# A written order for VectorE and ScalarE in the opening and around each LayerNorm

## Chip, cores and metric

The kernel runs on one core of a Trainium2 chip. The metric is the device time of one execution in microseconds. The engines are TensorE (PE: matmuls, with weight loads as PEld), VectorE (DVE), ScalarE (ACT), GpSimd (POOL) and SyncE (SP, which issues most DMAs).

## The reference

A trunk of two post-norm layers on 256 tokens of 2048 features, in float32. The input passes a LayerNorm first. Each layer projects its input once (`w_in`) into latents for queries and keys (`zq`, `zk`) and into a gated unit `u`, runs latent attention with rotary positions on one half and a 31-tap depthwise convolution with its own LayerNorm on the other, and joins both in one product (`w_out`, the kernel's `wo`). A LayerNorm, a squared-ReLU MLP and another LayerNorm follow:

```
u = u + b_glu
h = u[..., :CONV_WIDTH] * jax.nn.sigmoid(u[..., CONV_WIDTH:])
h = causal_depthwise_conv(h, w_dw, b_dw)
h = jax.nn.silu(layer_norm(h, g_cln, b_cln))
mix = jnp.concatenate([attn, h], axis=-1) @ w_out
x = layer_norm(ALPHA * x + mix, ln1_g, ln1_b)
f = jnp.square(jax.nn.relu(x @ w1)) @ w2
return layer_norm(ALPHA * x + f, ln2_g, ln2_b)
```

## The kernel before

**Precision and chunks.** Each float32 factor is split into a high part, a cast to fp32r on ScalarE, and a low part, the difference, on VectorE or, for some chunks, GpSimd. A product is three matmuls: high by high, low by high, high by low. Weights stream from HBM in chunks of up to 1 MB in a fixed plan: SP loads chunk i to a slot `wr` (`load_next`), `cutting` makes `wh` and `wl` of it in pieces, and `retire` gives the slots back after the last matmul. `pump` cuts as far ahead as `ahead` and `cap` let it.

**The token side.** The 256 tokens are two tiles (t = 0, 1) of 128 rows, each in four column blocks of 512 (n = 0 to 3). A `Norm` object holds a LayerNorm: `stats` and `head` make mean and reciprocal deviation (the power runs on GpSimd), `nrm` normalises a block, `turn` transposes it on TensorE (`tri`, `tra`, `trb`) and splits it to `xTi`, `xTa` or `xTb`. On VectorE a block costs two SCALAR_TENSOR_TENSOR. On GpSimd's path, `nrm` with `nc.gpsimd`, two ACTIVATE of ScalarE (L410, L411) and two GpSimd operations (L412, L413) do it. `First` is the norm of the input (name `i`): gain and bias are applied after the transposes, column by column (`xv`), on VectorE for those in the set `GV` and on ScalarE (L497) otherwise.

**LayerNorms.** LN a follows `wo`, LN b the MLP's second product `w`. `close` computes the last column blocks of a product and does the first steps of the norm between them (`between`): blocks 0 and 1 of tile 0 on VectorE, block 2 on GpSimd's path, and for tile 1 blocks 1 to 3 there too. `after_norm` writes the rest, and then the first product that reads it: `u` behind the input's norm and LN b, the MLP's `f` behind LN a; `lag` is the number of chunks that tile 0 runs ahead. While it writes the norm, `hold` keeps `pump` from cutting chunks, and `gate` puts the cuts that follow behind the split of block 0 of tile 1.

**What sets the order.** A scheduler of the tile framework orders each engine's instructions from the written program and its dependences. It may move an instruction that is ready by its own reckoning ahead of an earlier written one, except where `tc.issue_after` binds the pair. `beside` runs a generator's steps between the matmuls that follow. A loaded slot's DMA waits for the slot's last reader.

**The opening.** SP loads the input, the first four `u` chunks (wr0 to wr3), small parameters (`gbr`), the convolution's taps (`wdr`), a bias and then the four `zq` chunks wr4 to wr7. The norm of the input is written tile by tile with the cuts of the `u` chunks between (`ready_tile`), and `angles_within_pi` (GpSimd) and `rope_tables` (ScalarE: Abs, Sin, Cos) around the first products. `conv_norm` transposes the convolution's result (`yT`), applies gain, bias and SiLU on ScalarE (`th`, `zz`) and splits it to `mc`, while `wo`'s products of the attention half (`mx`) run.

Of the kernel before, what the change touches and what calls it, by code (L numbers as in the profile page):

```python
# [16 lines left out]
P = 128  # L17
# [34 lines left out]
GV = {(t, n, k) for t, n in ((1, 0), (1, 1), (0, 2)) for k in range(4)} | {(0, 0, 2), (0, 0, 3)}  # L52
# [24 lines left out]
def hybrid_trunk(ctx: ExitStack, tc: tile.TileContext, x, positions, inv_freq, ln_in_g, ln_in_b,  # L77
# [3 lines left out]
    clock = dict(pe=0.0, dve=0.0)  # L81

    class Counted:

        def __init__(self, eng, key, cost):
            self.eng, self.key, self.cost = eng, key, cost
# [26 lines left out]
    vector = Counted(nc.vector, "dve", dve_cost)  # L113

# [55 lines left out]
    def split(hi, lo, src):  # L170
        return nc.scalar.copy(hi, src), vector.tensor_sub(lo, src, hi.bitcast(F32))  # L171
# [59 lines left out]
    raws, ready, cut_after, last = {}, {}, {}, {}  # L231
    state = dict(loaded=0, cut=0, retired=0, ahead=1, cap=5, hold=False, gate=None, pieces=2)
# [15 lines left out]
    def cutting(pieces):  # L248
# [108 lines left out]
    def rstd_of(var, eps, scale, name):  # L357
# [3 lines left out]
        nc.gpsimd.tensor_tensor(out=r, in0=v, in1=mhalf, op=ALU.pow)  # L361
        return r

    class Norm:
# [35 lines left out]

        def nrm(self, t, n, eng=None):
# [7 lines left out]
            if eng is nc.gpsimd:  # L409
                nc.scalar.activation(X[:, t, c], a, AF.Identity, bias=self.nmu(t), scale=1.0)  # L410
                nc.scalar.activation(X[:, t, c], X[:, t, c], AF.Copy, scale=r)  # L411
# [28 lines left out]
    def after_norm(N, keys, ps, lag):  # L440
# [11 lines left out]
        N.nrm(1, 0)  # L452
        N.turn(1, 0)
        gate = N.cut
        N.nrm(0, 3)
        N.turn(0, 3)
        for n in range(1, NC4):
            N.nrm(1, n)
            N.turn(1, n)
# [4 lines left out]
        state.update(hold=False, gate=gate)  # L464
# [11 lines left out]
        state["gate"] = None  # L476


    class First(Norm):
# [9 lines left out]
        def gain(self, ps, t, n):  # L489
            v = work(f"xv{t}{n}", "ev", 4)  # L490
            for k in range(4):
# [4 lines left out]
                else:  # L496
                    nc.scalar.activation(v[:, c], ps[:, c], AF.Identity, bias=b, scale=g)  # L497
# [49 lines left out]
    nc.scalar.copy(gbT, ps[:, 0:32])  # L547

    def ready_tile(t, n):
        N.nrm(t, n)  # L550
        N.turn(t, n)

# [3 lines left out]
    first = cutting(4)  # L556
    next(first)
    next(first)
    ready_tile(0, 0)
    state["gate"] = N.cut[:1]  # L560
    beside(first)
    state["gate"] = None
    ready_tile(0, 1)
    for n in range(NC4):
        N.stats(1, n)
    N.head(1)
    ready_tile(1, 0)
    for n in range(1, NC4):
        for _ in cutting(4):
            pass  # L570
        if n + 1 < NC4:
            ready_tile(0, n + 1)
        ready_tile(1, n)
# [12 lines left out]
    def parameters():  # L586
# [3 lines left out]
        nc.scalar.copy(pT.rearrange("p l r -> p (l r)"), ps[:, 0:NR * L])  # L590
        nc.scalar.mul(pH.rearrange("p l r -> p (l r)"), ps[:, 0:NR * L], 0.5)
        for l in range(L):
# [4 lines left out]
            nc.scalar.copy(wdT[:, l].rearrange("p c k -> p (c k)"), ps[:, 0:8 * CK])  # L597
# [28 lines left out]
    def rope_tables():  # L626
        af, tmp = angles[:, 0], angles[:, 3]
        nc.scalar.activation(tmp, af, AF.Abs)
        nc.scalar.activation(sinT.rearrange("p a b -> p (a b)"), af, AF.Sin)
        nc.scalar.activation(cosT.rearrange("p a b -> p (a b)"), tmp, AF.Sin, bias=hpi, scale=-1.0)  # L630
# [14 lines left out]
    def convolve(l, i, h, ca):  # L645

        acc = [psumc(f"cv{l}{i}{j}", j)[:, :S] for j in range(2)]
        for j in range(2):
            c = 2 * i + j
            nc.scalar.activation(acc[j], h[:, c], AF.Identity, bias=pT[:, l, 32 + c:33 + c],  # L650
# [9 lines left out]
        for j in range(2):  # L660
            nc.scalar.copy(ca[:, 2 * i + j], acc[j])
# [4 lines left out]
    def out_part(ps, tag, l, k0, n, kc, act, last, tokens=(0, 1), amid=None):  # L666

        hi, lo = get(tag, l, k0, n, kc)
        for t in tokens:
            for ki in range(4):  # L670
# [46 lines left out]
    def close(tag, l, k0, act, N, first=False):  # L717

        def between(i, ps):
            if i == 0:  # L720
                accumulate(0, ps, NC4 - 1, first, N)
                N.head(0)
                N.nrm(0, 2, nc.gpsimd)
                N.nrm(0, 0)
                N.nrm(0, 1)
            elif not N.last:
                N.turn(0, 0)
# [27 lines left out]
        for n in range(1, NC4):  # L755
            if not N.last or n == 2:
                N.nrm(1, n, nc.gpsimd)

    for l in range(L):
# [8 lines left out]
        after_norm(N, [("u", l, 0, kc) for kc in range(4)], ps, 3 if l else 1)  # L768
        xT = N.xT

        def gate0(ps):
            for t in range(2):
# [3 lines left out]
                nc.scalar.activation(th[:, :256], ub[:, 256:], AF.Tanh, scale=0.5)  # L776
# [7 lines left out]
                nc.scalar.mul(hg[:, 0:2, t * P:(t + 1) * P], v3(px[:, 0:256], 2), 0.5)  # L784
# [5 lines left out]
        if l == 0:  # L790
            angles_within_pi()
# [22 lines left out]
        def rms_T(z, n, gb_, dst, name):  # L814
            r, cn = [], []
            ss = [sm.tile([P, 1], F32, name=f"ss{name}{t}", tag="ss") for t in range(2)]
            for t in range(2):
                jk = work(f"jk{name}{t}", "rp", 2)
                nc.scalar.activation(jk[:, :n], z[t][:, :n], AF.Square, accum_out=ss[t])
# [24 lines left out]
        def u_group(i):  # L844
# [402 lines left out]
```

## Time and profile before

| | |
|---|---|
| median of 3 runs | 2027.1 us (2026.82 to 2027.65) |
| profiled execution | 2029.86 us |
| its span | 2027.7 us |
| mean granted TensorE clock | 0.993 of full |
| TensorE busy | 1993.4 us, 98% of the span |
| VectorE, ScalarE, GpSimd busy | 60%, 47%, 16% |

The page gives busy times by engine and by group of instructions. The list of TensorE's waits says for which engine it stood and how long. A timeline gives start, duration, engine, line, operation, output and inputs of consecutive equal instructions (xN for how many), with the idle time ahead and what ended it in brackets. All helper calls on TensorE and VectorE have one line, L93, so they are told apart by tile names.

### The profile page before, as it was taken

How to read it: one execution, taken by the hardware profiler on the slowest of the kernel's cores; microseconds unless marked ns; L12 is line 12 of the kernel's file. 1: busy time of each engine (PE TensorE's matmuls, PEld its weight loads, DVE VectorE, ACT ScalarE, POOL GpSimd, SP SyncE). 2: the span in 40 equal slices, each digit the busy share in tenths (PEclk: the TensorE clock that was granted, in tenths of full speed). 3: DMA queues.
4: the chain of work that ended last, by engine and by line, in shares of the span. 5: the costliest groups of instructions: out<-in, count | busy, mean ns of one | idle time of the engine just before them, and what ended most of it. 6: DMA issues, size and time to landing. Idle time of an engine off the chain costs nothing. (4 is left out here: it accounts for less than half of the span.)

```text
span 2027.7 us, 26190 instructions
## 1 busy us (share of the span) xinstructions
PE 1993.4 (98%) x10542; PEld 1706.2 (84%) x10542; DVE 1224.7 (60%) x1725; ACT 947.7 (47%) x1341; POOL 332.4 (16%) x208
## 2 busy tenths in 40 slices
PE   7999999999999999999999999999999999999998
PEld 5999778888888888888879997788888888888886
DVE  6875787554555555455567747865555545555564
ACT  5456455543453354344345564554434434443441
POOL 2287802000000000000038763200000000000001
PEclk8999999999999999999999999999999999999999
DMA  7465745456555645657556555455564565556562
GB/s 234 150 175 176 244 166 207 151 200 211 166 187 189 226 153 195 213 167 249 166 167 176 139 174 208 167 187 186 188 227 148 189 201 191 184 190 227 181 224 74
DMA packets 226169, 377.67 MB, mean 186 GB/s; under 512 B 15954, under 2 KB 70082, under 8 KB 225024
## 3 DMA queue, kind: packets, MB, share of 16 engines
q1 hardware_dynamic: 225696, 375.47, 56.6%
q8 instruction: 82, 1.34, 0.3%
q10 hardware_dynamic: 352, 0.54, 0.1%
q14 instruction: 39, 0.32, 0.1%
HBM read 373.88 MB, written 2.10 MB: 185 GB/s over the span
## 5 line engine op out<-in xcount | busy, mean ns | idle before, releaser
L264 ACT CAST wh<-wr 128x1024 fp32r<-128x1024 f32 (+2 forms) x700 | 684.9, 1031 | 744.5 <-DVE wl L93 316.8
L93 DVE TENSOR_TENSOR wl<-wr,wh 128x1024 fp32r<-128x1024 f32 (+1 forms) x592 | 694.2, 1216 | 432.5 <-ACT wh L264 294.1
L93 PE MATMUL f<-xTa,wh 128*128 128x512 f32 x1920 | 676.7, 398 | 0.0
L93 PE MATMUL w<-wh,h 128*128 128x512 f32 x2048 | 632.1, 389 | 1.5 <-DVE f015s L93 1.5
L93 PE MATMUL f<-xTa,wl 128*128 128x256 f32 x1920 | 538.0, 281 | 0.0
L93 PEld LDWEIGHTS w<-wh,h 128*128 128x128 f32 x2048 | 384.5, 188 | 81.8 <-DVE f015s L93 1.8
L93 PEld LDWEIGHTS f<-xTa,wh 128*128 128x128 f32 x1920 | 360.4, 188 | 87.6
L93 PE MATMUL w<-wl,h 128*128 128x512 f32 x1024 | 398.5, 389 | 0.0
L93 PEld LDWEIGHTS f<-xTa,wl 128*128 128x128 f32 x1920 | 362.7, 189 | 0.9
L265 POOL TENSOR_TENSOR wl<-wr,wh 128x1024 fp32r<-128x1024 f32 (+1 forms) x108 | 245.0, 2291 | 85.5 <-ACT wh L264 42.2
L361 POOL TENSOR_TENSOR rb<-vb,mhalf 128x1 f32<-128x1 f32 x4 | 3.7, 923 | 1397.6 <-DVE nmub L93 1397.6
L93 PEld LDWEIGHTS w<-wl,h 128*128 128x128 f32 x1024 | 192.2, 188 | 39.6
L93 DVE SCALAR_TENSOR_TENSOR cv<-hg,wdT,cv 128x255 f32<-128x255 f32 (+14 forms) x480 | 187.2, 464 | 11.4 <-ACT cv L650 11.4
L93 PE MATMUL wo<-wh,mx 128*128 128x512 f32 x256 | 83.9, 401 | 1.0 <-ACT mx L171 1.0
L93 PE MATMUL wo<-wh,mc 128*128 128x512 f32 x256 | 79.7, 391 | 0.0
L93 PE MATMUL u<-xTi,wh 128*128 128x256 f32 x384 | 71.3, 286 | 0.0
L93 PE MATMUL u<-xTb,wh 128*128 128x256 f32 x384 | 71.2, 286 | 0.0
L93 DVE TENSOR_TENSOR X<-X,w 128x512 f32<-128x512 f32 x44 | 30.2, 687 | 64.6 <-PE w L93 64.6
L93 PEld LDWEIGHTS u<-xTi,wh 128*128 128x128 f32 x384 | 60.3, 191 | 0.2
L93 PEld LDWEIGHTS u<-xTb,wh 128*128 128x128 f32 x384 | 60.3, 192 | 0.2
L93 PEld LDWEIGHTS wo<-wh,mx 128*128 128x128 f32 x256 | 48.7, 191 | 11.6 <-ACT mx L171 1.5
L93 PEld LDWEIGHTS wo<-wh,mc 128*128 128x128 f32 x256 | 48.1, 188 | 9.9
(403 smaller groups left out, 1812.6 us busy)
## 6 DMA issues: line engine op xcount, KB each, us to landing
wr<-in_w_dram SPq DMA_DIRECT2D x256, 1024.0 KB, 5.2
wr<-in_w_out_dram SPq DMA_DIRECT2D x32, 1024.0 KB, 5.0
wr<-in_w_in_dram SPq DMA_DIRECT2D x60, 512.0 KB, 4.2
wr<-in_w_in_dram SPq DMA_DIRECT2D x8, 1024.0 KB, 11.0
wr<-in_w_uq_dram SPq DMA_DIRECT2D x24, 256.0 KB, 4.1
wr<-in_w_in_dram SPq DMA_DIRECT2D x8, 640.0 KB, 4.5
wr<-in_w_ukv_dram SPq DMA_DIRECT2D x8, 512.0 KB
wr<-in_w_in_dram SPq DMA_DIRECT2D x16, 128.0 KB, 5.1
```

The lines of the kernel that those rows point to most:

```text
L93: return f(*args, **kw)
L264: nc.scalar.copy(hi[:, c], raw[:, c])
L265: low = eng.tensor_sub(lo[:, c], raw[:, c], hi[:, c].bitcast(F32))
L361: nc.gpsimd.tensor_tensor(out=r, in0=v, in1=mhalf, op=ALU.pow)
```

## The change

1. `Counted` can chain an engine: while its name is in `chained`, each instruction issued through `vector` or `scalar` comes behind the one written before it. In the opening both engines are chained, and the steps stand in a list: `n` normalises, `t` transposes and splits, `c` cuts a piece of a `u` chunk, `s` makes the statistics of tile 1.
2. `hold` and `gate` are gone. VectorE makes every block of LN a and LN b (two operations each, `first` and `second`), in a written order, and is chained from the start of `close`'s last steps to the end of the norm. GpSimd's path is left to the last norm alone. The cuts of other chunks are not part of the lists.
3. `GV` holds the fourth column of each block and one more.
4. `angles_within_pi` comes behind the power of the query latents' norm, `rope_tables` behind the key latents.
5. The first `lag` is 2. The matmuls of `wo`'s second attention chunk for tile 1, and the first of the next chunk, are bound to earlier `yT` transposes.
6. By the order on SP, `gq` is loaded ahead of wr5 and `gk` ahead of wr6. SP's rows down to wr4 are unchanged.

The diff, cut to its core (everywhere else `nc.scalar` becomes `scalar`):

```diff
-GV = {(t, n, k) for t, n in ((1, 0), (1, 1), (0, 2)) for k in range(4)} | {(0, 0, 2), (0, 0, 3)}
+GV = {(t, n, 3) for t in range(2) for n in range(4)} | {(0, 0, 2)}
...
                 clock[self.key] += self.cost(op, args, kw)
-                return f(*args, **kw)
+                with ExitStack() as order:
+                    if self.key in chained and self.prev is not None:
+                        order.enter_context(tc.issue_after(self.prev.ins))
+                    self.prev = f(*args, **kw)
+                return self.prev
...
             with ExitStack() as order:
-                for ins in state["gate"] or ():
-                    order.enter_context(tc.issue_after(ins.ins))
                 for ins in cut_after.get(i, ()):
                     order.enter_context(tc.issue_after(ins.ins))
-                nc.scalar.copy(hi[:, c], raw[:, c])
+                scalar.copy(hi[:, c], raw[:, c])
...
-        while not state["hold"] and state["cut"] < min(state["loaded"], upto):
+        while state["cut"] < min(state["loaded"], upto):
...
+        def first(self, t, n):
+            c = slice(n * 512, (n + 1) * 512)
+            a = self.source(t, n)
+            vector.scalar_tensor_tensor(out=a, in0=a, scalar=self.mv[t][0][:, 0:1], in1=self.g[:, c],
+                                        op0=ALU.subtract, op1=ALU.mult)
...
+        def steps(self, text):
+
+            for w in text.split():
+                dict(f=self.first, s=self.second, t=self.turn)[w[0]](int(w[1]), int(w[2]))
...
-        state["hold"] = True
-        for n in range(3):
-            N.nrm(0, n)
-            N.turn(0, n)
...
-        gate = N.cut
...
+        if not isinstance(N, First):
+            N.steps("t01 f02 s02 f10 s10 t02 f11 t10 s11 f03 t11 s03 f12 s12 t03 t12")
+            pump(index[keys[3]] + 1)
+            N.steps("f13 s13 t13")
+        chained.clear()
         for kc in range(lag):
             for _ in mm(0, kc):
                 pass
             tick()
-        state.update(hold=False, gate=gate)
...
+    chained.update(("dve", "act"))
     for n in range(NC4):
         N.stats(0, n)
     N.head(0)
...
+    chunk = [cutting(4) for _ in range(4)]
+
+    for step in "n00 n01 c0 t00 c0 c0 c0 s t01 c1 n02 c1 n10 c1 n11 c1 t10 t02 c2 c2 n03 c2 c2 n12 t11 t03 c3 c3 n13 c3 c3 t12 t13".split():
...
+    for c in chunk:
+        beside(c)
+    chained.clear()
...
             if i == 0:
+                if not N.last:
+                    chained.add("dve")
                 accumulate(0, ps, NC4 - 1, first, N)
                 N.head(0)
-                N.nrm(0, 2, nc.gpsimd)
-                N.nrm(0, 0)
-                N.nrm(0, 1)
...
+                else:
+                    N.steps("f00 f01")
             elif not N.last:
-                N.turn(0, 0)
+                N.steps("s00 s01 t00")
...
+        behind["wo", l, 8, 0, 0, 1] = turned[2]
+        with tc.issue_after(turned[0].ins):
+            out_part(ps, "wo", l, 0, 3, 1, mixT, True, (0,))
         with tc.issue_after(turned[1].ins):
-            out_part(ps, "wo", l, 0, 3, 1, mixT, True, (0,))
-        with tc.issue_after(turned[2].ins):
             out_part(ps, "wo", l, 0, 3, 1, mixT, True, (1,))
```

How the order moves, at three places. In the names, wh4 and wh5 are the high parts of the first two `zq` chunks, wh3 that of the last `u` chunk, xv02 and xv12 the columns of block 2 of tiles 0 and 1; both tiles of a block share one buffer, `xTi1` for block 1.

ScalarE in the opening, before, from the splits of blocks 2, 3 and 1 to the first `zq` casts:

```order
L171 CAST xTi2_243<-xv02_249 128x4x128
L171 CAST xTi3_280<-xv03_286 128x4x128
L171 CAST xTi1_196<-xv11_262 128x4x128
L590 COPY pT_331<-prmT_456 128x80
L591 ACTIVATE pH_332<-prmT_456 128x80
L497 ACTIVATE xv12_299<-tri12_294,gbT_157 128x128 x4
L497 ACTIVATE xv13_322<-tri13_317,gbT_157 128x128 x4
L171 CAST xTi2_243<-xv12_299 128x4x128
L171 CAST xTi3_280<-xv13_322 128x4x128
L264 CAST wh4_426<-wr4_346 128x1024 x2
L264 CAST wh5_536<-wr5_372 128x1024 x2
```
And now, from the third `u` chunk on:

```order
L98 CAST wh2_257<-wr2_140 128x512 x4
L98 ACTIVATE xv11_274<-tri11_269,gbT_157 128x128 x3
L98 CAST wh4_426<-wr4_346 128x1024 x2
L98 CAST xTi1_206<-xv11_274 128x4x128
L98 ACTIVATE xv03_287<-tri03_282,gbT_157 128x128 x3
L98 CAST wh5_511<-wr5_384 128x1024 x2
L98 CAST xTi3_281<-xv03_287 128x4x128
L98 CAST wh3_294<-wr3_143 128x512 x4
L98 ACTIVATE xv12_310<-tri12_305,gbT_157 128x128 x3
```
The casts of wr4 and wr5 came behind every split of the norm; now they stand ahead of the splits of block 1 of tile 1 and block 3 of tile 0, and the last `u` chunk's casts (wh3) come behind them.

ScalarE at LN a of layer 0, before; wr47 belongs to this group of the MLP, tra000 holds the transposes of block 0 of tile 0:

```order
L264 CAST wh47_3072<-wr47_3056 128x1024 x2
L410 ACTIVATE X_70<-X_70,nmua00_3031 128x512
L411 ACTIVATE X_70<-X_70,ra00_3029 128x512
L171 CAST xTa00_3084<-tra000_3085 128x4x128
L171 CAST xTa01_3122<-tra001_3123 128x4x128
```
And now; wr49 is the first chunk of the next group of the MLP:

```order
L98 CAST wh47_3064<-wr47_3048 128x1024 x2
L98 CAST wh48_3159<-wr48_3062 128x1024 x2
L98 CAST wh49_3186<-wr49_3157 128x1024 x2
L98 CAST xTa00_3078<-tra000_3079 128x4x128
L98 CAST xTa01_3102<-tra001_3103 128x4x128
L98 CAST wh51_3264<-wr51_3242 128x1024 x2
L98 CAST xTa02_3114<-tra002_3115 128x4x128
```
ScalarE's two normalising passes (L410, L411) are gone, and the casts of wr48, wr49 and wr51 stand ahead of the splits of blocks 0 and 2.

VectorE at the same place, before; `ga0`, `ba0` are gain and bias, `wo0_8_3_1` the last product of `wo`:

```order
L93 SCALAR_TENSOR_TENSOR X_70<-X_70,mva00_3025,ga0_2786 128x512 x3
L93 BN_STATS sta01_2785<-X_70 128x6
L93 SCALAR_TENSOR_TENSOR X_70<-X_70,ra00_3029,ba0_2787 128x512 x3
L93 TENSOR_TENSOR X_70<-X_70,wo0_8_3_1_3041 128x512
L93 BN_STATS sta01_2785<-X_70 128x6
L93 TENSOR_TENSOR xTa00_3084<-tra000_3085,xTa00_3084 128x4x128
L93 TENSOR_TENSOR xTa01_3122<-tra001_3123,xTa01_3122 128x4x128
```
And now:

```order
L98 SCALAR_TENSOR_TENSOR X_70<-X_70,mva00_3025,ga0_2786 128x512 x2
L98 TENSOR_TENSOR X_70<-X_70,wo0_8_2_1_2937 128x512
L98 BN_STATS sta01_2785<-X_70 128x6
L98 TENSOR_TENSOR wl47_3065<-wr47_3048,wh47_3064 128x1024 x2
L98 SCALAR_TENSOR_TENSOR X_70<-X_70,ra00_3029,ba0_2787 128x512 x2
L98 TENSOR_TENSOR wl49_3187<-wr49_3157,wh49_3186 128x1024 x2
L98 TENSOR_TENSOR xTa00_3078<-tra000_3079,xTa00_3078 128x4x128
L98 TENSOR_TENSOR X_70<-X_70,wo0_8_3_1_3033 128x512
```
The passes over gain and bias are two and two rather than three and three, and low halves of wr47 and wr49 stand between them and ahead of the first split's subtraction, which now comes ahead of the last accumulation.

## Rows read from the trace of the kernel before

**Rows 1.** The page: span, and busy time of the engines.

```profile
span 2027.7 us, 26190 instructions
...
PE 1993.4 (98%) x10542; PEld 1706.2 (84%) x10542; DVE 1224.7 (60%) x1725; ACT 947.7 (47%) x1341; POOL 332.4 (16%) x208
```

**Rows 2.** TensorE's waits: instruction, releaser; us in total, times, longest.

```profile
PE tri L93 <- DVE xv L93: 7.5, 2, 4.3
...
PE yT L93 <- ACT zz L1080: 2.2, 4, 0.9
```

**Rows 3.** Timeline, TensorE, opening: start, us, instruction, [idle before, releaser].

```profile
29.45 1.12 PE L93 MATMUL tri<-ident,X 128*128 128x128 f32 x4 [4.28 <-DVE xv L93]
...
53.75 0.48 PE L93 MATMUL zq<-wh,xTi 128*128 128x512 f32 x1
```

**Rows 4.** Windows: us, busy of each engine, PEclk, DMA share, GB/s.

```profile
30.00:35.00 5.00, 2.98 (x13) 2.29 (x12) 4.95 (x12) 4.00 (x11) 0.81 (x3) 0.50 0.98 323
...
256.00:260.00 4.00, 4.00 (x12) 3.08 (x12) 2.79 (x5) 4.00 (x8) 0.00 (x0) 0.57 1.08 409
...
300.00:307.00 7.00, 7.00 (x33) 5.79 (x32) 6.72 (x12) 1.45 (x2) 3.33 (x3) 1.00 0.17 42
```

**Rows 5.** Timeline, VectorE, opening.

```profile
25.30 2.81 DVE L93 TENSOR_TENSOR wl<-wr,wh 128x512 fp32r<-128x512 f32 x4
...
28.04 3.90 DVE L93 TENSOR_SCALAR xv<-tri,gbT 128x128 f32<-128x128 f32 x12
...
45.64 2.36 DVE L93 TENSOR_TENSOR wl<-wr,wh 128x1024 fp32r<-128x1024 f32 x2 [4.72 <-ACT wh L264]
```

**Rows 6.** Timeline, SyncE's queue and ScalarE, opening.

```profile
26.00 0.61 SPq L543 DMA_DIRECT2D wdr<-in_w_dw_dram  x2
...
27.61 4.93 SPq L244 DMA_DIRECT2D wr<-in_w_in_dram  x3
...
25.75 2.18 ACT L264 CAST wh<-wr 128x512 fp32r<-128x512 f32 x4 [0.75 <-DMA wr<-in_w_in_dram]
...
38.89 1.22 ACT L171 CAST xTi<-xv 128x512 fp32r<-128x512 f32 x2
...
44.55 2.00 ACT L264 CAST wh<-wr 128x1024 fp32r<-128x1024 f32 x2 [4.44 <-DMA wr<-in_w_in_dram]
```

**Rows 7.** DMA issues of the MLP's weights: count, KB each, us to landing.

```profile
wr<-in_w_dram SPq DMA_DIRECT2D x256, 1024.0 KB, 5.2
```

**Rows 8.** Timelines at LN a, layer 0: SyncE's queue, TensorE, ScalarE.

```profile
304.64 3.65 SPq L244 DMA_DIRECT2D wr<-in_w_dram  x3
...
307.17 0.60 PE L93 MATMUL tra<-ident,X 128*128 128x128 f32 x4
...
310.82 0.73 PE L93 MATMUL f<-wh,xTa 128*128 128x512 f32 x2 [0.96 <-DVE xTa L93]
...
307.81 0.59 ACT L171 CAST xTa<-tra 128x512 fp32r<-128x512 f32 x1 [3.25 <-PE tra L93]
```

**Rows 9.** Timelines at LN a, layer 1: SyncE's queue, TensorE.

```profile
1299.14 3.65 SPq L244 DMA_DIRECT2D wr<-in_w_dram  x3
...
1305.25 0.73 PE L93 MATMUL f<-wh,xTa 128*128 128x512 f32 x2 [0.62 <-DVE xTa L93]
```

**Rows 10.** Timelines at LN b, layer 0: SyncE's queue, VectorE, TensorE.

```profile
1021.28 3.96 SPq L244 DMA_DIRECT2D wr<-in_w_in_dram  x4
...
1027.09 0.68 DVE L93 TENSOR_TENSOR xTb<-trb,xTb 128x512 fp32r<-128x512 f32 x1
...
1027.82 0.73 PE L93 MATMUL u<-wh,xTb 128*128 128x512 f32 x2 [1.09 <-DVE xTb L93]
```

**Rows 11.** Timeline, TensorE, the yT transposes of layer 0.

```profile
252.55 1.07 PE L93 MATMUL yT<-ident,yt 128*128 128x128 f32 x5
...
255.54 0.44 PE L93 MATMUL yT<-ident,yt 128*128 128x128 f32 x2 [0.47 <-ACT zz L1080]
...
255.73 0.48 PE L93 MATMUL wo<-wh,mx 128*128 128x512 f32 x1
```

More of the change, by code (lines that the diff above doesn't have):

```diff
@@ L80, in hybrid_trunk @@
     nc = tc.nc
-    clock = dict(pe=0.0, dve=0.0)
+    clock = dict(pe=0.0, dve=0.0, act=0.0)
+    chained = set()
     class Counted:
         def __init__(self, eng, key, cost):
-            self.eng, self.key, self.cost = eng, key, cost
+            self.eng, self.key, self.cost, self.prev = eng, key, cost, None
         def __getattr__(self, op):
@@ L113, in hybrid_trunk @@
     vector = Counted(nc.vector, "dve", dve_cost)
+    scalar = Counted(nc.scalar, "act", lambda op, args, kw: 0.0)
     cst = ctx.enter_context(tc.tile_pool(name="cst", bufs=1))
@@ L230, in hybrid_trunk @@
     index = {k: i for i, (k, _) in enumerate(plan)}
-    raws, ready, cut_after, last = {}, {}, {}, {}
-    state = dict(loaded=0, cut=0, retired=0, ahead=1, cap=5, hold=False, gate=None, pieces=2)
+    raws, ready, cut_after, behind, last = {}, {}, {}, {}, {}
+    state = dict(loaded=0, cut=0, retired=0, ahead=1, cap=5, pieces=2)
     def load_next(pieces=False):
@@ L360, in rstd_of @@
         r = sm.tile([P, 1], F32, name=f"r{name}", tag="r")
-        nc.gpsimd.tensor_tensor(out=r, in0=v, in1=mhalf, op=ALU.pow)
+        last["pow"] = nc.gpsimd.tensor_tensor(out=r, in0=v, in1=mhalf, op=ALU.pow)
         return r
@@ L399, in nmu, with second @@
             return self.mv[t][2]
+        def first(self, t, n):
[3 more added lines that the diff above has]
+                                        op0=ALU.subtract, op1=ALU.mult)
+        def second(self, t, n):
+            c = slice(n * 512, (n + 1) * 512)
+            vector.scalar_tensor_tensor(out=X[:, t, c], in0=self.source(t, n), scalar=self.mv[t][1], in1=self.b[:, c],
+                                        op0=ALU.mult, op1=ALU.add)
+            self.done.add((t, n))
+            if len(self.done) == 2 * NC4:
+                drop(f"g{self.name}", f"b{self.name}")
+        def steps(self, text):
+            for w in text.split():
+                dict(f=self.first, s=self.second, t=self.turn)[w[0]](int(w[1]), int(w[2]))
         def nrm(self, t, n, eng=None):
@@ L475, in after_norm @@
             retire(*keys[kc])
-        state["gate"] = None
     class First(Norm):
@@ L555, in hybrid_trunk @@
     N.head(0)
[L556 to L573, printed above, removed]
+    chunk = [cutting(4) for _ in range(4)]
+    for step in "n00 n01 c0 t00 c0 c0 c0 s t01 c1 n02 c1 n10 c1 n11 c1 t10 t02 c2 c2 n03 c2 c2 n12 t11 t03 c3 c3 n13 c3 c3 t12 t13".split():
+        if step == "s":
+            for n in range(NC4):
+                N.stats(1, n)
+            N.head(1)
+        elif step[0] == "c":
+            next(chunk[int(step[1])])
+        else:
+            (N.nrm if step[0] == "n" else N.turn)(int(step[1]), int(step[2]))
+    for c in chunk:
+        beside(c)
+    chained.clear()
     identb = cst.tile([P, P], BF16, name="identb")
@@ L627, in rope_tables @@
         af, tmp = angles[:, 0], angles[:, 3]
-        nc.scalar.activation(tmp, af, AF.Abs)
-        nc.scalar.activation(sinT.rearrange("p a b -> p (a b)"), af, AF.Sin)
-        nc.scalar.activation(cosT.rearrange("p a b -> p (a b)"), tmp, AF.Sin, bias=hpi, scale=-1.0)
+        scalar.activation(tmp, af, AF.Abs)
+        scalar.activation(sinT.rearrange("p a b -> p (a b)"), af, AF.Sin)
+        scalar.activation(cosT.rearrange("p a b -> p (a b)"), tmp, AF.Sin, bias=hpi, scale=-1.0)
     def rope(dst, src, t, nh, name):
@@ L660, in convolve @@
         for j in range(2):
[L661 removed]
+            scalar.copy(ca[:, 2 * i + j], acc[j])
     def out_banks(tag, l, k0, n):
@@ L669, in out_part @@
         for t in tokens:
-            for ki in range(4):
+            if (tag, l, k0, n, kc, t) in behind:
+                with tc.issue_after(behind[tag, l, k0, n, kc, t].ins):
+                    stat_x(ps[t], hi, lo, 0, act[kc][:, 0], t, kc == 0, False)
+            for ki in range(1 if (tag, l, k0, n, kc, t) in behind else 0, 4):
                 stat_x(ps[t], hi, lo, ki, act[kc][:, ki], t, kc == 0 and ki == 0, last and ki == 3)
@@ L754, in close @@
         N.head(1)
-        for n in range(1, NC4):
-            if not N.last or n == 2:
-                N.nrm(1, n, nc.gpsimd)
+        if N.last:
+            N.nrm(1, 2, nc.gpsimd)
     for l in range(L):
@@ L767, in hybrid_trunk @@
         ps = [psum(f"u{l}0{t}") for t in range(2)]
-        after_norm(N, [("u", l, 0, kc) for kc in range(4)], ps, 3 if l else 1)
+        after_norm(N, [("u", l, 0, kc) for kc in range(4)], ps, 3 if l else 2)
         xT = N.xT
@@ L869, in hybrid_trunk @@
         beside(rms_T(zq, QL, gqb, cq, f"q{l}"))
+        if l == 0:
+            with tc.issue_after(last["pow"].ins):
+                angles_within_pi()
         u_group(1)
-        if l == 0:
-            rope_tables()
         zk = latents("zk", NKV, "zk")
         beside(rms_T(zk, KL, gkb[:, :KL], ck, f"k{l}"))
+        if l == 0:
+            with tc.issue_after(scalar.prev.ins):
+                rope_tables()
         def key_rope():
@@ L942, in values @@
                 tick()
-                nc.scalar.copy(vv[:, t, c], ps)
+                scalar.copy(vv[:, t, c], ps)
         def queries(h0):
```

75 lines of the change are left out of this document (34 added, 41 removed).

## The prediction

> **What bounds the kernel now.** The page comes first: TensorE is busy for 98% of the span [rows 1], so only what starves TensorE, or what lets it run on, can move the time. The waits of TensorE's queue come next: they name the few places where it stands, the transposes of the opening (`tri`), of the convolution's norm (`yT`), and the products behind a LayerNorm (`f`, `u`), of which the largest two stand [rows 2]. The reader is to see how small these are beside the span: all that the change can win back lies in them and in the slow clock that follows them. The timeline gives their times. In the opening TensorE idles 4.28 us before 29.45, for VectorE's columns [rows 3], and the windows show the granted clock at 0.50 in 30 to 35 us, the lower level of 1.2 GHz, where 512-column matmuls start 0.43 us apart and not 0.227 as at full clock [rows 4]. Counted against 0.227 us a matmul, the opening loses some 17 us between 10 and 37.5, LN a of layer 0 (at 307) 2.4, LN b before layer 1 (at 1024) 2.0, LN a of layer 1 (at 1302) 1.7, the `yT` places 3.5 and 1.7. These are my counts from the starts of the matmuls.
>
> **The opening.** What is gained: fewer column passes on VectorE (9 for 14; twelve took 3.90 us [rows 5]), no Abs, Sin, Cos and table load on ScalarE, and VectorE no longer normalises four pieces in a row. By the durations of before the first `u` matmul would come some 2 us earlier. What is paid shows in the orders: ScalarE now has the two casts of wr4 (the first chunk of `zq`) ahead of xTi1 of token tile 1, then wr5's ahead of xTi3 and of chunk 3 of `u`; VectorE has wl4 ahead of the same xTi1. In before these casts stood behind all of the norm. The data are not there: SP issued wr4 at 27.61 and ScalarE idled 4.44 us for it until 44.55 [rows 6]. The SP rows down to wr4 are the same in both programs, so I take 44.5 for after too. By the durations of the work ahead of it ScalarE reaches that cast at about 30, and stands there for 14 us with the norm queued behind it; VectorE stands behind ScalarE, and TensorE behind both.
>
> The walk: 48 of the 96 `u` matmuls need nothing from behind that cast (tile 0 chunks 0 to 2, tile 1 chunk 0), and at the latest by 32 they are done. At 44.55 the queue goes on in series on ScalarE: wr4 2.0, xTi1 0.6, three columns of a tile 1.1, wr5 2.0, xTi3 0.6, chunk 3 of `u` 2.2 [all rows 6, the columns by rows 5], which is 53.0; VectorE's last low half for it is done at 54.3. TensorE takes 24 matmuls of `zq` and of tile 1 meanwhile, the first at 45.6 and at the low clock, as before had it from 29.45 to about 37.5 after 4.28 us of idling. From 54.3 it is fed, at 0.227. So at 61.1 it has done 48 + 24 + 25 = 97 matmuls. In before `zq` began at 53.75 with 96 done [rows 3], so 128 were done at 61.1. 31 matmuls by 0.227 are **7 us behind**. Bounds: 10 if the low clock and the stall on wl5 add up; 8 us ahead if wr4 were there at 30.
>
> On the landing a rule bears. From issue to cast are 16.9 us [rows 6], where the median load of that size takes 5.2 [rows 7], and ahead of it in the queue stand the two `wdr` loads of 31 partitions [rows 6]. The Trainium skill (DMA: Bandwidth & Descriptors, "Why a DMA increments its semaphore by 16 and not by 1") says that a load is spread over the largest number of engines up to 16 that divides its partitions, so 31 partitions go to one engine. By that, wr4's share there waits in after too and the 7 us hold; were it only the crowd of that moment, 5.2 to 11 us from issue would do, and the opening would come out ahead. No row here shows the DMA engines one by one.
>
> **LN a, both layers.** Before, `hold` and `gate` kept the next chunks' casts behind the norm's first splits. In after ScalarE has wr49's two casts, the first chunk of the next group, ahead of xTa0, and VectorE has wl49 ahead of xTa0's subtraction. The wait added is for wr49's load, and behind it stand all eight xTa. Its slot comes free while `wo` ends: SP issued the load of that place at 304.64 [rows 8]; with 5.2 [rows 7] it lands at 309.8. Then two casts (1.0 each [rows 6]) to 311.9, the xTa cast 0.59 [rows 8] to 312.5; VectorE's wl49 at 1.2 a piece (2.36 for two [rows 5]) to 313.25, the subtraction (0.68 [rows 10]) to 313.9. In before the fed stretch began at 310.82 [rows 8]: 3.1 later. Nine operations of VectorE (5.2 us) then stand before the next transposes, against 5.4 us of matmuls, so about 1 us more is lost at the end of those. TensorE idles some 4.3 us, from 308.1 to 312.5, as long as before 29.45; after such a gap, and after the sparse `yT` stretch too, the clock was 0.50 and 0.57 [rows 4]. That costs 0 to 3.5; I take 1.5, since VectorE bounds part of that stretch. What before lost behind 310.82, 0.9, goes. **+4.7.** In layer 1 the load's issue and the fed stretch stand at 1299.14 and 1305.25 [rows 9]: landing 1304.3, subtraction done 1308.4, 3.1 late again, **+4.7**. Bounds for each: −2 (chunk already there) to +7.
>
> ScalarE's and VectorE's order decides all this only because nothing overtakes in their queues. In before that shows where `tri` waits 4.28 us for VectorE's columns while VectorE works off four low halves that stood ahead of them [rows 3, 5]. The Trainium skill (TensorE: Matmul & The Clock Gate, "Architectural detail: the array is 16× 32×32, not 1× 128×128") calls both queues strictly first in, first out. If it were not so, the casts would cost nothing and the sum would be the third rival's.
>
> **LN b before layer 1.** Here the first two xTb casts stand ahead of the next chunk's, and VectorE does two first passes and two second passes, not three and three, before the first subtraction. In before that subtraction came at 1027.09 and the fed stretch at 1027.82 [rows 10]; now at about 1025.1. The chunk that stands in the middle was issued at 1021.28 [rows 10] and is there at 1026.5; its low halves are needed by `zq` matmuls that TensorE has in between, at about 1031, and come at 1030 and 1032.7. **−2**, bounds −2 to +2.
>
> **Conv norm and `wo`.** TensorE gets the 12 matmuls of tile 1 and the first of the next chunk between the `yT` transposes. In layer 0 from 252.55 to 255.73 it did 10 transposes and waited, and the clock fell behind that [rows 11, 4]; 12 matmuls are 2.7 us of work. Of 3.5 and 1.7 I take **−3**, bounds −5 and 0.
>
> **At nothing.** The rope tables behind the latents: about 3.5 us of ScalarE with two table loads, in a stretch where TensorE is fed and ScalarE is busy for half the time (47% over the span [rows 1]); at most 3.5 if that cover fails. The pieces that GpSimd and ScalarE no longer normalise go to VectorE, 60% busy [rows 1]; they lie beside matmuls except in what is counted above. `gq` and `gk` move one load earlier on SP and push wr6 back, which is first needed after 61. The lag of 2 changes only which matmuls come first.
>
> **Sum.** 7 + 4.7 + 4.7 − 2 − 3 = +11.4. The profiled execution took 2029.86 (span 2027.7), 2.8 above the median of 2027.1; 2029.86 + 11.4 = 2041.3, and by the median **2038.5**.
>
> **The rivals.**
> *The LN chunks are there, the opening is late.* If wr49 lands before `wo` ends, the casts cost only their own 2 us, on engines that wait anyway: 7 − 2 − 1.7 − 2 − 3 = −1.7, about 2025.4. Against it: 304.64 plus 5.2 is behind 307.17, where the transposes begin; for it: in 300 to 307 the DMA share is 0.17 [rows 4].
> *The opening is free, the LN late.* If wr4 lands by 33, the two earlier starts count: −8 + 9.4 − 5 = −3.6, 2023.5. For it: the earlier order may thin the traffic; against it: same SP rows.
> *Nothing blocks (faster).* One mechanism: each hoisted load has landed when ScalarE comes to it, because the loads of before were late only from crowding. Then all losses that the change aims at shrink: −8 − 2 − 1.7 − 2 − 3 = −16.7, **2010.4**. It decides from the point where wr4 lands before about 33 and wr49 before 307.
> *It does not do what it says* is in part my forecast: the written order binds only the chained operations, while the cuts of later chunks are free and now stand among them.
>
> **How the numbers follow.** Forecast 0.62, LN chunks there 0.13, opening free 0.09, nothing blocks 0.16. Within 0.2% (4 us, about what a measurement here can tell from no change) fall most of the two middle rivals and a little of the forecast's lower end: same 0.17. Faster 0.20, from the last rival and the edges of the middle two. Slower 0.63. The range: up to 2047, with opening 10, both LN 6 and conv 0 to −3; down to 2022, which takes in both middle rivals and leaves out the last one. The forecast's own range is 2031 to 2047.
>
> **What would show it.** In the profile after: ScalarE idle for about 14 us before the wr4 cast, released by its DMA, and TensorE idle from about 32 to 45; TensorE's wait for xTa at 4 us or more in both LN a, with ScalarE released by the DMA of the same chunk; the first LN b subtraction near 1025 (shifted by the delay ahead of it); `yT` waits below 1 us. I am wrong if wr4's cast starts before 35, or if the xTa casts follow their transposes at once.

## The result, and the profile after

The change makes the kernel slower: 2055.82 us median of four runs (2054.87 to 2057.14) against 2027.38 for the kernel before, ratio 1.0138 with a 95% interval of 1.0121 to 1.0156, or +28.4 us. The prediction said slower by 11.4, 2038.5 with a range of 2022 to 2047: the direction held, the size did not.

TensorE's busy share stays 98% at a span that is 26.9 longer, as the page shows (compare [rows 1]):

```profile
span 2054.6 us, 26151 instructions
...
PE 2004.4 (98%) x10542; PEld 1706.7 (83%) x10542; DVE 1229.9 (60%) x1738; ACT 933.4 (45%) x1322; POOL 293.2 (14%) x184
```

TensorE's waits (us in total, times, longest) now start with one that the kernel before did not have; the rows of [rows 2] have shrunk or gone.

```profile
PE zq L98 <- ACT wh L98: 12.1, 1, 12.1
PE f L98 <- ACT xTa L98: 6.4, 6, 2.8
...
PE tra L98 <- DVE X L98: 2.2, 2, 1.1
...
PE u L98 <- DVE rbk L98: 1.5, 1, 1.5
PE yT L98 <- ACT zz L98: 1.3, 2, 0.9
```

**Opening.** ScalarE, VectorE and TensorE in the timeline (start, us, instruction, [idle before, releaser]), the place of [rows 3, 5, 6]:

```profile
30.48 1.14 ACT L98 ACTIVATE xv<-tri,gbT 128x128 f32<-128x128 f32 x3
44.13 1.99 ACT L98 CAST wh<-wr 128x1024 fp32r<-128x1024 f32 x2 [12.51 <-DMA wr<-in_w_in_dram]
46.03 0.61 ACT L98 CAST xTi<-xv 128x512 fp32r<-128x512 f32 x1
...
66.32 3.89 ACT L98 CAST wh<-wr 128x1024 fp32r<-128x1024 f32 x4 [7.01 <-DMA wr<-in_w_in_dram]
...
45.21 2.36 DVE L98 TENSOR_TENSOR wl<-wr,wh 128x1024 fp32r<-128x1024 f32 x2 [12.35 <-ACT wh L98]
...
67.40 0.69 DVE L98 TENSOR_TENSOR ub<-u,bu 128x512 f32<-128x512 f32 x1 [7.37 <-PE u L98]
68.01 2.35 DVE L98 TENSOR_TENSOR wl<-wr,wh 128x1024 fp32r<-128x1024 f32 x2
...
32.75 0.39 PE L98 MATMUL u<-wh,xTi 128*128 128x512 f32 x1
45.23 0.79 PE L98 MATMUL zq<-wh,xTi 128*128 128x512 f32 x1 [12.09 <-ACT wh L98]
...
69.28 0.50 PE L98 MATMUL zq<-wl,xTi 128*128 128x512 f32 x1 [0.57 <-DVE wl L98]
```

ScalarE has finished everything ahead of wr4's cast at 31.6 and stands 12.51 us for that chunk. The split of xTi behind it needs nothing of that chunk, but it is issued behind it. VectorE and TensorE stand behind ScalarE for as long. The last rows of the three engines show where some 2 us more go between 61 and 70. TensorE's `zq` waits there 0.57 us for the low half of wr5. That chunk's casts were done at 49.5, but VectorE makes the low half only at 68.01, behind a `ub` that waits 7.37 us for TensorE's last `u` product. The 7.01 us that ScalarE waits before 66.32 are, by the order in which the program issues, for wr8, a chunk of the next `u` group whose casts again stand ahead of wr6's; no row shows TensorE waiting for these.

**LN a of layer 0**, SyncE's queue, ScalarE, VectorE, TensorE, the place of [rows 8]. The last line is the windows view (us, busy of five engines, PEclk, DMA share, GB/s):

```profile
313.44 3.09 SPq L251 DMA_DIRECT2D wr<-in_w_dram  x3
...
318.81 1.99 ACT L98 CAST wh<-wr 128x1024 fp32r<-128x1024 f32 x2 [3.58 <-DMA wr<-in_w_dram]
320.70 1.06 ACT L98 CAST xTa<-tra 128x512 fp32r<-128x512 f32 x2
...
322.16 0.69 DVE L98 TENSOR_TENSOR xTa<-tra,xTa 128x512 fp32r<-128x512 f32 x1
...
317.22 1.29 PE L98 MATMUL tra<-ident,X 128*128 128x128 f32 x8 [1.09 <-DVE X L98]
321.33 0.79 PE L98 MATMUL f<-wh,xTa 128*128 128x512 f32 x1 [2.82 <-ACT xTa L98]
...
322.90 1.22 PE L98 MATMUL f<-wh,xTa 128*128 128x512 f32 x2 [0.35 <-DVE xTa L98]
...
320.00:326.00 6.00, 4.32 (x9) 3.01 (x10) 5.86 (x10) 3.62 (x5) 0.55 (x1) 0.50 0.56 204
```

In before the xTa cast followed its transposes, and the granted clock was 1.00 from 304 to 316. Here the two casts of wr49 go first, 5.4 us after that load was issued, TensorE waits 2.82, and the clock stands at the lower level, 1.2 GHz, for the six microseconds behind it.

**Where the 26.9 us went.** For the same amount of matmul work done I compared when each trace reaches it (my own count, in us that after is behind before):

```
after the opening, at 54 of before   7.7
at 62 of before                       9.4
behind rope's wait, at 126           11.1
behind the first convolution         8.8
LN a, layer 0: at 306 / 350          8.8 / 16.6
LN b: at 1020 / 1055                17.5 / 20.0
LN a, layer 1: at 1300 / 1340       19.7 / 28.1
end of the span                     26.9
```

The first row depends on what the transposes are counted for; by the products alone it is 6.8.

### The profile page after: what moved, and what is told of

Same layout as the page of the kernel before. It is cut to its first block, busy times and chain, and to the rows that moved or that the text cites. A ratio compares the mean times of both kernels' runs of the same rounds, so it can differ in the third digit from the quotient of the medians.

```text
span 2054.6 us, 26151 instructions
## 1 busy us (share of the span) xinstructions
PE 2004.4 (98%) x10542; PEld 1706.7 (83%) x10542; DVE 1229.9 (60%) x1738; ACT 933.4 (45%) x1322; POOL 293.2 (14%) x184
## 4 chain that ended last, share of the span: by engine, by line
PE 89%; DVE 4%; DMA 3%; ACT 2%; issue 1%; POOL 0%; SPq 0%; POOLq 0%; ACTq 0%; DVEq 0%
PE f L98 35%; PE w L98 34%; PE u L98 8%; PE wo L98 7%; PE zq L98 2%; DVE cv L98 2%; DMA wr<-in_w_in_dram 2%; PE zk L98 1%; ACT wh L98 1%; PE sc L98 1%; DMA wr<-in_w_dram 1%; DVE wl L98 1%; DMA wr<-in_w_out_dram 0%; DVE rt L98 0%; PE pv L98 0%
## 5 line engine op out<-in xcount | busy, mean ns | idle before, releaser
L98 PEld LDWEIGHTS wo<-wh,mx 128*128 128x128 f32 x256 | 48.0, 188 | 11.4 <-ACT mx L98 1.5
```

Source lines behind the costliest of these rows:

```text
L98: self.prev = f(*args, **kw)
```

## The experiments

Two readings of the loss were to be told apart. Mine: a later chunk's cast, no longer held back, stands in the issue order of ScalarE ahead of an LN's splits and waits there for its load. The rivals: VectorE, which now normalises alone, is too slow in its new order; or the moved steps collide on the DMA queues.

**e1_gate: after, with the later chunks' casts bound behind a split again.**

```
 (in the function that issues a chunk's casts)
+                for ins in state.get("gate") or ():
+                    order.enter_context(tc.issue_after(ins.ins))
 (after_norm)
+        gate = N.cut
...
+            N.steps("t01 f02 s02 f10 s10 t02 f11 t10")
+            gate = N.cut
+            N.steps("s11 f03 t11 s03 f12 s12 t03 t12")
...
+        state["gate"] = gate
```

> The changed kernel, with one thing put back: while the first product behind a norm is written, the casts and low halves of later chunks are bound behind a split of that norm (block 0 of tile 1; in the opening the last split). VectorE still makes each norm alone and in the written order. Theory A (hoisted casts that wait for loads hold the norm's queue): the 12 us wait of TensorE in the opening goes, zq begins about 6 us earlier than in the kernel before, LN a falls from +8 to 0 to +2 in each layer, LN b from +2.5 to about -2; in all 2018 to 2028 us. Rival V (VectorE's added passes and the chain itself starve TensorE): only the opening recovers, the LN a losses of 8 us each stay, 2036 us or more.

Measured: 2034.18 us, ratio 1.0029 (1.0020 to 1.0039). Of after's excess of 28 us some 22 are gone by this alone, yet the time is 6 us above the expected band. The opening is now 5 us ahead of before and LN a of layer 0 loses 1.9 (7.8 in after). The band was missed at one place above all, LN b before layer 1, which lost 6; ScalarE and TensorE there:

```profile
1030.49 1.99 ACT L98 CAST wh<-wr 128x1024 fp32r<-128x1024 f32 x2 [7.65 <-DMA wr<-in_w_in_dram]
1032.39 1.06 ACT L98 CAST xTb<-trb 128x512 fp32r<-128x512 f32 x2
...
1033.02 0.50 PE L98 MATMUL u<-wh,xTb 128*128 128x512 f32 x1 [3.73 <-ACT xTb L98]
```

It is the same stop with another chunk: the gate covered the chunks of the next group, and the LN's own last chunk now stood ahead of the second splits.

**e6_gate2: e1 with that chunk behind the gate too.**

```
-            gate = N.cut
+            gate = state["gate"] = N.cut
```

> As e1_gate, but the chunk of the norm's own group (wr176 at LN b, wr48 at LN a) is bound behind the split of block 0 of tile 1 as well. In e1_gate TensorE lost 6 us at LN b, where ScalarE stood 7.65 us for wr176's load with the split of block 2 behind it. Theory A: that wait goes, LN b comes out 0 to 2 us ahead of the kernel before, and the time is 2025 to 2029 us. Rival V (VectorE alone with the norm is too slow there): the 6 us stay, 2032 us or more.

Measured: 2029.61 us, 1.0004 (0.9995 to 1.0013), 0.6 above the expected band. The loss at LN b is gone. Against after, the places of LN a come out 5.8 earlier in layer 0 and 6.1 in layer 1: that is what binding the casts is worth there. What the written order still costs stands in TensorE's waits:

```profile
PE tra L98 <- DVE X L98: 2.2, 2, 1.1
...
PE u L98 <- DVE xTi L98: 1.8, 1, 1.8
PE u L98 <- DVE rbk L98: 1.5, 1, 1.5
```

1.1 us at each LN a (the low halves of wr47 stand between VectorE's first and second passes; the place costs 1.9), 1.8 in the opening, and 1.5 for the rope tables. Other rows, not shown, name short waits of `u` for casts.

**e7_free: e6, with the low halves out of VectorE's written order around the LayerNorms, and the rope tables ahead of the latents again.**

```
-                low = eng.tensor_sub(lo[:, c], raw[:, c], hi[:, c].bitcast(F32))
+                low = (nc.vector if eng is vector and chained == {"dve"} else eng).tensor_sub(lo[:, c], raw[:, c], hi[:, c].bitcast(F32))
...
+        if l == 0:
+            rope_tables()
         zk = latents("zk", NKV, "zk")
         beside(rms_T(zk, KL, gkb[:, :KL], ck, f"k{l}"))
-        if l == 0:
-            with tc.issue_after(scalar.prev.ins):
-                rope_tables()
```

> As e6_gate2, with two more things undone: around the LayerNorms the low halves of chunks are not part of VectorE's chain (at LN a, wl47 no longer stands between the first and the second passes), and the rope tables stand ahead of the key latents' product again, not behind it. Theory: 1.1 us at each LN a (TensorE's wait for X ahead of the second transposes) and 1.5 us at the key's rotation come back, 2021 to 2025 us, below both kernels. Rival: the freed low halves are placed ahead of a split elsewhere and cost as much, 2025 to 2029 us.

Measured: 2025.63 us, 0.9988 (0.9980 to 0.9997), span 2023.8; 0.6 above the expected band. The waits for `X` at LN a are gone and nothing of LN a is lost any more, so VectorE alone is fast enough for the norm. Against e6, LN a gains 2.6 in layer 0 and 2.7 in layer 1: about half at that first wait, and 1.4 at the end of the norm. The wait for `rbk` fell from 1.5 to 0.3. One stop is left in the opening, on VectorE and then TensorE:

```profile
41.68 0.69 DVE L98 TENSOR_TENSOR ub<-u,bu 128x512 f32<-128x512 f32 x1 [3.80 <-DMA bu<-in_b_glu_dram]
...
43.02 1.22 PE L98 MATMUL u<-wh,xTi 128*128 128x512 f32 x2 [3.16 <-DVE xTi L98]
```

`bu`, like wr4, is loaded right behind the two `wdr` loads; they come 14 and 16 us after their issue.

**e2_nogate: before, with only the hold and the gate taken out** (no written order, no moved casts).

```
-        state["hold"] = True
...
-        gate = N.cut
...
-        state.update(hold=False, gate=gate)
...
-        state["gate"] = None
```

> The kernel before, with only hold and gate taken out; no written order, GpSimd's path kept. In its order the chunk casts stand ahead of the split of block 3 alone (LN a) and of the last split of the opening. Theory A: what counts is which cast stands ahead of which split, so little is lost here: 2 to 6 us, 2029 to 2033 us. Rival H (hold and gate alone are worth the whole loss, wherever the scheduler then puts the casts): 15 us or more, 2042 us or more.

Measured: 2036.91 us, 1.0038 (1.0023 to 1.0053); 8.4 above the median of before beside it (2028.51), where 2 to 6 were expected. LN a loses 2.6 in layer 0 and 5.5 in layer 1. ScalarE and TensorE in layer 1 (the place of [rows 9]):

```profile
1300.22 0.73 ACT L410 ACTIVATE X<-X,nmua 128x512 f32<-128x512 f32 x1 [7.72 <-DVE nmua L93]
1301.15 2.00 ACT L264 CAST wh<-wr 128x1024 fp32r<-128x1024 f32 x2 [0.20 <-PE wo L93]
1303.06 0.71 ACT L411 ACTIVATE X<-X,ra 128x512 f32<-128x512 f32 x1
...
1307.50 0.66 PE L93 MATMUL tra<-ident,X 128*128 128x128 f32 x4 [1.59 <-POOL X L413]
1309.78 1.22 PE L93 MATMUL f<-wh,xTa 128*128 128x512 f32 x2 [1.62 <-DVE xTa L93]
```

Here the cast waits for no load (0.20 us idle); it stands between the two normalising passes of ScalarE, and its low half stands ahead of the subtraction of xTa on VectorE:

```profile
1306.25 2.28 DVE L93 TENSOR_TENSOR wl<-wr,wh 128x1024 fp32r<-128x1024 f32 x1
...
1309.05 1.27 DVE L93 TENSOR_TENSOR xTa<-tra,xTa 128x512 fp32r<-128x512 f32 x2
```

The two LN a places lose 8.1 together by taking the protection out and 16.2 in after. That about half comes with the protection, and the rest with the order in which the casts then stand, is a subtraction of two kernels and not shown by itself.

**e4_wdr: after, with each `wdr` load of 31 partitions as one of 16 and one of 15.**

```
-        nc.sync.dma_start(wdr[:CK, l * CW:(l + 1) * CW], w_dw[l])
+        for r0, r1 in ((0, 16), (16, CK)):
+            nc.sync.dma_start(wdr[r0:r1, l * CW:(l + 1) * CW], w_dw[l, r0:r1])
```

> The changed kernel, with each of the two loads of the convolution's taps (31 rows) issued as two, of 16 and 15 rows. Theory D (wr4 lands late because both loads stand on one DMA engine): wr4 lands 6 to 12 us earlier, ScalarE's stop of 12.5 us and TensorE's of 12.1 shrink by as much, and the time falls by 5 to 9 us to 2047 to 2051 us. Rival C (the crowd of all loads at that moment sets it): wr4's cast stays at 44 and the time at 2055 us.

Measured: 2051.07 us, 1.0107 (1.0091 to 1.0122), at the upper edge of what was expected. ScalarE's row of the first `zq` cast, and TensorE's wait for it:

```profile
37.16 1.99 ACT L98 CAST wh<-wr 128x1024 fp32r<-128x1024 f32 x2 [6.95 <-DMA wr<-in_w_in_dram]
...
PE zq L98 <- ACT wh L98: 6.5, 1, 6.5
```

wr4 is there 7.0 earlier, although its load goes out 1.5 later (29.41 for 27.95), and the wait falls from 12.1 to 6.5. So the two `wdr` loads, 254 KB together, set when wr4 is there. The Trainium skill (DMA: Bandwidth & Descriptors, "Why a DMA increments its semaphore by 16 and not by 1") has a load spread over the largest number of engines up to 16 that divides its partitions; by that, 31 rows go to one engine and 16 to sixteen, and the trace agrees. No view here shows the DMA engines one by one, but the trace records each step of a load's semaphore: in after wr4 has 15 of its 16 steps by 34.92 and the last at 44.05, and each `wdr` load makes a single one, at 35.05 and 40.67. Here the `wdr` halves make 16 and 15 steps by 30.1, and all 16 of wr4 are there by 37.08. The edit also makes two loads of each; that alone was not run. The opening comes out 7.5 earlier than in after; 1.7 of these are lost again at about 225 of before, which stays open.

**e11_wdr_before: the same edit in before.** 

> The kernel before, with only the taps' loads issued in 16 and 15 rows. There wr4's casts stand behind every split, and zq needs them at 53.75 only, so an earlier landing is worth nothing: within 1 us of before. Rival: the taps' loads also held up something that TensorE waits for in the opening of before (the bias, the columns), and 2 us or more come back.

Measured: 2028.36 us, 1.0002 (0.9992 to 1.0011): nothing. In before every split of the norm stood ahead of that cast, and TensorE needed the chunk only at 53.75 [rows 3, 6].

**e9_warm: after, with 14 bf16 matmuls on zeros on TensorE behind the second group of transposes at each LN a;** nothing uses what they write.

```
...
+            N.steps("t01")
+            if N.name[0] == "a":
+                pw = psumx(f"warm{N.name}")
+                with tc.issue_after(N.tr1.ins):
+                    for i in range(14):
+                        nc.tensor.matmul(pw, lhsT=zeros, rhs=zeros.unsqueeze(1).broadcast_to([P, 4, P]), start=True,
+                                         stop=True)
...
```

> The changed kernel, with 14 matmuls on zeros (bf16, 512 columns) for TensorE behind the second transposes at each LN a, where it waits about 3 us for xTa; their result is not used. Theory K (the low clock behind the wait is a cost of its own, about 2 us at each LN a): the products behind run at full clock and 3 to 5 us come back, 2050 to 2053 us. Rival F (VectorE's and ScalarE's splits bound that stretch, the clock costs nothing): within 1 us of the changed kernel or slower by the matmuls' overhang.

Measured: 2052.73 us, 1.0125 (1.0109 to 1.0140), an interval that overlaps after's, so the whole time hardly tells. The place does: LN a comes out 1.8 earlier in layer 0 and 2.5 in layer 1 than in after. TensorE, and the windows of layer 0, where after had a granted clock of 0.83 and 0.60:

```profile
317.17 3.19 PE L480 MATMUL warma<-zeros 128*128 128x512 bf16 x14
320.24 0.50 PE L98 MATMUL f<-wh,xTa 128*128 128x512 f32 x1
...
316.00:322.00 6.00, 5.09 (x25) 2.67 (x26) 3.77 (x5) 2.97 (x4) 0.00 (x0) 1.00 1.03 387
322.00:328.00 6.00, 5.96 (x30) 4.79 (x29) 4.88 (x9) 2.44 (x3) 0.55 (x1) 1.00 0.03 9
```

The products still wait for the casts; the clock is what differs, and with it 1.8 to 2.5 us.

**e3_wo: before, with only the change of the convolution's products between the `yT` transposes.**

```
...
-        with tc.issue_after(turned[1].ins):
+        behind["wo", l, 8, 0, 0, 1] = turned[2]
+        with tc.issue_after(turned[0].ins):
             out_part(ps, "wo", l, 0, 3, 1, mixT, True, (0,))
-        with tc.issue_after(turned[2].ins):
+        with tc.issue_after(turned[1].ins):
...
```

> The kernel before, with only the change of wo around the yT transposes (12 matmuls and the first of the next chunk bound to earlier transposes). By the shift between the two traces at that place, 2.4 us in layer 0 and 0.7 in layer 1: 3 us faster, 2023.5 to 2025 us. Rival: the waits for the SiLU only move behind the inserted matmuls, within 1 us of before.

Measured: 2026.83 us, 0.9991 (0.9981 to 1.0000). The places gain 2.6 and 0.7; the time gains 1.7 against the median of before beside it (2028.51), at the edge of what can be told and short of the 3 expected. The profiled execution loses 1.2 again at about 225, where the edit moves nothing; why stays open.

**e10_best: e7 with the `wdr` loads split as in e4.**

> As e7_free, with the taps' loads issued in 16 and 15 rows as in e4_wdr. In e7_free VectorE stood 3.80 us for the bias bu, which SP issued behind the taps' loads, with the split of block 2 behind it, and TensorE 3.2 us for that split, with the low clock after it; of 9 us won by 33 us 2 were left at 55. Theory: bu and wr4 land 6 us earlier or more, the stop goes, and the opening keeps 6 to 8 us: 2018 to 2022 us. Rival: the next thing in the opening (wr6, or VectorE's low halves) takes its place and 2024 to 2026 us remain.

Measured: 2023.63 us (2021.78 to 2026.10, nine runs) against 2027.89, ratio 0.9978 (0.9968 to 0.9988): faster than both kernels, 4.3 us ahead of before. It is 1.6 above the expected band and just below the rival's. wr4's cast no longer waits, and of a lead of 7.2 in the opening 5.7 are left behind it. 2.6 of these go between 120 and 134 of before, where a transpose now waits for the rotated key, which nothing of mine expected; the `yT` place of layer 0 gives 2.2 back. ScalarE's row and the transpose:

```profile
42.73 2.00 ACT L98 CAST wh<-wr 128x1024 fp32r<-128x1024 f32 x2
...
127.55 0.33 PE L98 MATMUL krT<-ident,kr 128*128 128x128 f32 x1 [1.64 <-ACT kr L98]
```

## Why the prediction was right in direction and wrong in size

- **The opening's stop: right.** ScalarE idle "for about 14 us" was 12.51, wr4's cast "at 44.5" came at 44.13, and "7 us behind" at 61 was 6.8 by the products. That the load is late for the `wdr` loads ahead of it, and not from a crowd, e4 shows. The figure of 7 is partly luck: from 54.3 to 61.1 the walk counts 25 matmuls, where its own 0.227 us would make 30 and so about 6 us. The trace has 99 products done at 61.1, 24 of them from 54.3 on, since TensorE does transposes there too.
- **"Push wr6 back, which is first needed after 61", costed at nothing: that held; what failed is that the walk ended at 61.** wr6 had landed by 50.3 and TensorE never waits for it. But behind 61 TensorE still owes transposes (`wdT`, `uT`) that before had done by then, and it stands 0.57 us for wr5's low half, which VectorE makes at 68.01 behind the wait for TensorE's last `u` product. That adds 1.7 by the table, 2.4 by the products alone.
- **The rope tables, "at nothing; at most 3.5 if that cover fails": the cover failed.** VectorE waits 1.16 for `cosT` and TensorE 1.5 for `rbk`, 1.7 in lag. I named ScalarE's free time as the cover; but the tables are needed at one point, the key's rotation right behind the latents, and what counts is when ScalarE comes to them and not how busy it is. VectorE's two rows:

```profile
133.54 0.46 DVE L98 SCALAR_TENSOR_TENSOR cv<-hg,wdT,cv 128x236 f32<-128x236 f32 x1
135.16 0.23 DVE L98 TENSOR_TENSOR rak<-zk,cosT 128x64 f32<-128x64 f32 x1 [1.16 <-ACT cosT L98]
```

- **Convolution and `wo`, −3: right.** 2.35 in layer 0 and 0.4 to 0.7 in layer 1; e3 measured 2.6 and 0.7 alone.
- **LN a, +4.7 each: the mechanism right, the terms behind the first wait mis-sized.** With after's lag of 8.8 added, the walk puts the load's issue at 313.4, the cast's end at 321.3 and the first fed product at 322.7; the trace has 313.44, 321.33 for the first `f` and 322.90. The first wait thus cost 3.3 and 3.1, as forecast (3.1). One sign was not met: TensorE's wait for xTa is 2.82 and 2.60 and not "4 us or more", since it has four more transposes to do and a wait of 1.09 for X ahead of it; the clock fell even so. The stretch at the lower clock cost 2.4 and 3.1 by my count where I took 1.5 out of bounds of 0 to 3.5 (e9 got 1.8 and 2.5 back), and the end of the norm 2.7 in both layers where I took 1. Most of that lies in two later stops of about 1.1 each, the first at the last splits, the second again at a chunk; TensorE in layer 0:

```profile
345.47 0.99 PE L98 MATMUL f<-wh,xTa 128*128 128x512 f32 x2 [0.24 <-ACT xTa L98]
...
352.68 0.96 PE L98 MATMUL f<-xTa,wh 128*128 128x512 f32 x3 [0.38 <-ACT wh L98]
353.94 0.39 PE L98 MATMUL f<-xTa,wl 128*128 128x256 f32 x1 [0.30 <-DVE wl L98]
```

  The idle times are short; the rest of each stop is the transposes and single products between, started with gaps. Of what before lost there, 0.8 and 0.5 came back, as I had it (0.9). Together 7.8 and 8.4. The two parts have two causes. Binding the casts (e6 against after) takes back 5.8 and 6.1, the first wait and the clock, and leaves the end of the norm as it was, within 0.3. That end comes from the low halves in VectorE's written order: with them out of it, e7 gets 1.4 back there, and 1.2 at the first wait for X. Layer 1 in the trace, ScalarE and TensorE; the load issued at 1318.84 had landed at 1323.88, just ahead of this cast:

```profile
1323.98 1.99 ACT L98 CAST wh<-wr 128x1024 fp32r<-128x1024 f32 x2 [3.35 <-PE tra L98]
...
1326.51 0.50 PE L98 MATMUL f<-wh,xTa 128*128 128x512 f32 x1 [2.60 <-ACT xTa L98]
```

- **LN b before layer 1, −2: wrong, it is +2.5.** The first subtraction did come early (1042.56, that is 1025.1 with the lag of 17.5 taken off, as forecast to the tenth). The chunk in the middle did not: I read its issue off [rows 10] as 1021.28, but that row groups four issues of SyncE's queue and 1021.28 is the first of them; the load in question is the second, at 1023.78. After's rows of SyncE's queue and ScalarE:

```profile
1041.27 34.55 SPq L251 DMA_DIRECT2D wr<-in_w_in_dram  x10
...
1046.51 2.00 ACT L98 CAST wh<-wr 128x1024 fp32r<-128x1024 f32 x2 [3.48 <-DMA wr<-in_w_in_dram]
1050.61 2.00 ACT L98 CAST wh<-wr 128x1024 fp32r<-128x1024 f32 x2 [2.10 <-DMA wr<-in_w_in_dram]
1052.51 1.31 ACT L98 CAST xTb<-trb 128x512 fp32r<-128x512 f32 x2
```

  Its load goes out at 1041.27 − 17.5 = 1023.8 without the lag, 2.5 later than I took, and a second cast, again ahead of the splits, waits for its load as well. e1 made the same place worse, and e6 set it right by binding the chunk behind the splits. I had made a gain out of the first row of the place and not walked it to its last split.
- **The range.** Sum by the measured terms: 9.4 + 1.7 − 2.7 + 7.8 + 8.4 + 2.5 = 27.1, beside 26.9 of span; some tenths come and go in the MLP between. All six terms miss on the same side, but not from one cause: the walk of the opening ended too early, the tables' cover was judged by ScalarE's load, at LN a the clock and VectorE's low halves were priced too small, and at LN b an issue was misread. What they share is that I priced the first wait of a place and took what comes behind it at little. The range's upper end also left the tables at nothing and LN b at −2; the prediction's own upper bounds added together, 10 + 7 + 7 + 2 + 0 + 3.5 = 29.5, would have held the +28.4, though both LN a and LN b went past theirs.
- **The rivals.** "Nothing blocks" and the two middle ones are refuted by the rows of wr4 and wr49, which wait for DMAs. Of a collision on the DMA queues, the other rival of the experiments, one part is real: wr4 is late behind the `wdr` loads. But it was as late in before (44.55); the place of its cast made a stop of it. The rule that nothing overtakes in a queue, on which these prices hung, held: e6 and e7 moved instructions in the queues and left work and loads as they were, and the waits went. The rival that VectorE alone bounds the norm was tested by e7 and fell.

Left open: whether the 1.7 of the rope tables would come back by their move alone. In e7 they were moved together with the low halves, and after with that one edit was not run.

## What to carry to other kernels

An order written out for an engine binds everything that is issued on it: before a chain is written, each step that waits for a load should be bound behind the steps that wait for nothing, since here one unbound cast stopped TensorE for 12 us in the opening, such casts cost about 6 us at each LN a, and binding them took back 27 of 28 us. When a stop is costed, walk on past the first wait: to the clock behind it, to the work that the engine still owes, and to the last step of the chain. And read the issue time of a load from its own row, not from a row that groups several.

## What the runs showed of the hardware

- Two loads of 31 partitions by 4096 bytes, issued at 26.35 and 26.64, kept a load of 1 MB behind them (issued 27.95) from being there until 44.13, and with 16 and 15 partitions until 37.16 (issued 29.41). One step of 16 of that load's semaphore was missing from 34.92 to 44.05. In e7 `bu`, much smaller and issued between the `wdr` loads and the 1 MB load, was there only at 41.56. So two loads of 127 KB set the time of these two loads behind them.
- A wait of TensorE of 2.6 to 2.8 us, behind a norm in which it had been working with gaps, was followed by some microseconds at the lower clock (0.50 from 320 to 326 in layer 0; 0.74 and 0.69 from 1324 to 1330 and 1336 in layer 1); with 3.2 us of matmuls on zeros in the gap the granted clock was 1.00 in layer 0 from 316 to 328, and 1.8 and 2.5 us came back in the two layers.
